# A hybrid convolution and delta-rule layer: the mixer's intermediates move to PSUM banks, the decay series to VectorE, and the planner learns of a shared SBUF way

## The chip, the cores and the metric

The kernel runs on one core of a Trainium2 chip, in one launch. The metric is device time in microseconds (us), the median of several runs; one more execution was profiled. The engines are TensorE (PE), VectorE (DVE), ScalarE (ACT), GpSimd (POOL) and SyncE (SP, which issues most transfers).

## The reference

One layer over 2048 tokens of width 1024, in fp32: a modulated RMS norm, a mixer, a residual, a second norm, a gated feed-forward part, a final norm. The change touches the mixer:

```python
h = adaln(x, g_norm_mix[layer], shift_m, scale_m)
p = h @ w_in[layer]
gate_b, gate_c, h_conv, q, k, v, z, a, bt = jnp.split(p, split_at, axis=-1)
ya = gate_b * causal_depthwise_conv(gate_c * h_conv, conv_w_mix[layer])      # 3 taps
...                                                  # ya: RMS norm by groups of 64
qkv = jax.nn.silu(causal_depthwise_conv(jnp.concatenate([q, k, v], axis=-1), conv_w_qkv[layer]))  # 4 taps
...                                                  # q, k normalised; 4 heads of 128
beta = jax.nn.sigmoid(bt)
g_dec = -jnp.exp(a_log[layer]) * jax.nn.softplus(a + dt_bias[layer])
o = chunked_gated_delta_rule(q, k, v, g_dec, beta)
o = rms_norm(o, g_dn_out[layer]) * jax.nn.silu(z)
y = jnp.concatenate([ya, o], axis=-1) @ w_out[layer]
x = x + gate_m[:, None, :] * y
```

The delta rule keeps a 128x128 state for each head and steps over chunks: `v_new = u - w @ state`, `o = q @ state + attn @ v_new`, `state = state * exp(g_last) + k.T @ v_new`, where u and w come from the inverse of a unit lower triangular matrix for each chunk.

## The kernel before

A matrix product in fp32 is made of three fast ones (fp32r): high part by high, high by low, low by high. `split_w` makes `whi` (ACT cast) and `wlo` (DVE difference) of each weight strip; `scale_split` makes `hTh` and `hTl` of the normed, transposed rows. So a projection of a strip is 24 matmuls of 128x512 (`proj`, `dmm`), and these fill PE.

The mixer runs in four blocks of 512 tokens. A block projects four strips each of k, q, v and z, then 12 strips for the convolution half, and ends in the out-projection: two halves of 512 columns, each over four pairs of strips in the order `KPS`, where `ya` are the convolution's rows and `ybs` (tiles `ym`) the delta rule's. The first result of each four chunks of `ybs` is needed in the second pair of the first half. During it the next block's rows are transposed (`transpose_split`, pool `kq`).

Beside the projections, generators ("chains") issue all else. `head_chain` turns 16 columns of a and b (`ab2`), computes the decay g by a softplus series on [128 x 16] tiles, issues three small matmuls on g (L880 to L882), then one pair of matmuls on products `rg` for each head (L896), then `kT`'s. It goes on to a block inverse by recursion on DVE and transfers through DRAM. `level_chain` completes the inverse, `chunk_chain` steps over the chunks (`R`, `W`, `state`, `o`), `out_chain` norms o and turns it back (L1135). `mix_chain` norms the convolution half, `second_norm` reads the block before back, norms and turns it (L565), `mod_gen` and `to_row` (L485) make the modulation vectors, whose weight sums run on DVE (L444).

PSUM has eight banks in two pools of four, `pd` for projections and `pm` for the rest. `cv`, `lv` and `ch` are pools of SBUF tiles which chains take and give back.

What stands where is decided while the program is built. `Clock` estimates when each instruction ends: `fit` places it in a gap of its engine, `note` has the costs. After each third matmul `tick` resumes every chain whose next inputs `due` estimates as ready, plus 0.3 us. From the q strips of block 0 on, until the mixer's last out-projection, `order` and `pin` fix every engine's queue by the estimated start. Engines run their queues in order; transfers wait in SP's queue.

Of the kernel before, what the change touches and what calls it, by code (L numbers as in the profile page):

```python
# [53 lines left out]
class Clock:  # L54
# [15 lines left out]
    def fit(self, name, ready, cost):  # L70

        gaps = self.gaps[name]
        while len(gaps) > 1 and gaps[0][1] < self.pe - 60:
            gaps.pop(0)
        n = next(n for n, (a, b) in enumerate(gaps) if max(a, ready) + cost <= b)
        a, b = gaps[n]
        s = max(a, ready)
        gaps[n:n + 1] = [g for g in ([a, s], [s + cost, b]) if g[1] - g[0] > 0.02]
# [47 lines left out]
    def note(self, i):  # L126
# [9 lines left out]
        if op == "DMACopy":  # L136
            cost = min(a.free_size() * a.partition_size() for a in outs + ins) * 4 / 240e3
            begin = self.fit(eng, start, 0.45) - 0.45
            end = self.fit("DMA", begin + 1.2, cost) + 0.8
# [13 lines left out]
        else:  # L153
            if "Activation" in eng:
# [46 lines left out]
def layer_kernel(ctx, tc, x, c, w_ada, b_ada, w_ada_final, b_ada_final, g_norm_mix, g_norm_ffn, g_norm_final,  # L201
# [335 lines left out]
    def scale_split(ps, k, gcol, scol, hh, hl):  # L537
        ht = sp.tile([P, BLK], F32, name="ht", bufs=2)
        nc.scalar.activation(ht, ps, AF.Identity, scale=gcol[:, k:k + 1], bias=scol[:, k:k + 1])
        nc.vector.tensor_copy(hh[:, k, :], ht)  # L540
        nc.vector.tensor_sub(hl[:, k, :], ht, hh[:, k, :].bitcast(F32))  # L541
# [13 lines left out]
    def second_norm(b):  # L555
        for i in range(CH):
# [4 lines left out]
            for q in range(2):  # L561
                yield xt,
# [100 lines left out]
    with ExitStack() as actx:  # L663
        ap_ = Split(rctx, actx, {"hTh", "hTl", "kq", "kd", "vt", "zs", "E", "X", "lv", "ch", "Dg", "state"},
                    {"halo0", "halo1", "uhalo0", "uhalo1", "strict_r", "gones_r", "junkd", "nk", "nq", "sk",
# [117 lines left out]
        for b in range(NB):  # L783
# [18 lines left out]
            junkd = ap_.tile([P, BLK], mybir.dt.bfloat16, name="junkd")  # L802
# [28 lines left out]
            def head_chain(ps, b=b):  # L831
# [26 lines left out]
                nc.gpsimd.tensor_mul(zz, sg, sg)
                pl = t16("sp_p")
                nc.gpsimd.tensor_scalar(pl, zz, 1.0 / 17, 1.0 / 15, op0=ALU.mult, op1=ALU.add)  # L860
                for n in (13, 11, 9, 7, 5, 3, 1):
                    nc.gpsimd.tensor_mul(pl, pl, zz)
                    nc.gpsimd.tensor_scalar_add(pl, pl, 1.0 / n)
                nc.gpsimd.tensor_mul(pl, pl, sg)
                nc.scalar.activation(sy, sy, AF.Relu)
# [3 lines left out]
                nc.gpsimd.tensor_mul(g, pl, brd(nexpa))
# [16 lines left out]
                for h in range(NH):  # L886
# [6 lines left out]
                    yield tuple(rgs)  # L893
# [174 lines left out]
            def chunk_chain():  # L1068
# [5 lines left out]
                for j in range(CH):  # L1074
# [8 lines left out]
                    else:  # L1083
# [8 lines left out]
                        nc.vector.tensor_mul(R, h4(pks), bc(e_g, P))  # L1092
                        nc.vector.tensor_sub(R, vt[:, j], R)
# [25 lines left out]
            def out_chain(j, o):  # L1119
# [3 lines left out]
                for h in range(NH):  # L1123
                    nc.scalar.activation(junkd[:, hsl[h]], o[:, h, :], AF.Square, accum_out=so[:, h:h + 1])
# [7 lines left out]
                yield from take("ch", 1)  # L1132
# [3 lines left out]
                oT = ch_tile([P, NH, P])  # L1136
                nc.vector.scalar_tensor_tensor(oT, h4(pot), col["g_dn"], zs[:, :, j * P:(j + 1) * P],
# [17 lines left out]
            for key, c0, dstT in (("k", 2048, kT), ("q", 1536, qT), ("v", 2560, None)):  # L1155
                clock.pinned = clock.pinned or key == "q"
                for h in range(NH):
# [9 lines left out]
                    cb = ap_.tile([P, BLK + 3], F32, name="cb", bufs=2)  # L1167
                    nc.scalar.copy(cb[:, 3:], ps)
                    nc.vector.tensor_copy(cb[:, 0:3], halo[:, m, :])
# [3 lines left out]
                    tap = [col["cw_qkv"][:, t * 12 + m:t * 12 + m + 1] for t in range(4)]  # L1173
                    nc.vector.tensor_scalar_mul(cv, cb[:, 0:BLK], tap[0])
# [638 lines left out]
```

## Time and profile before

| | us |
|---|---|
| median of 3 runs | 2469.59 |
| lowest, highest | 2467.96, 2475.31 |
| profiled execution, time | 2471.74 |
| profiled execution, span | 2470.0 |
| PE busy | 2358.7 |
| DVE busy | 1809.0 |
| ACT busy | 1043.2 |
| POOL busy | 654.8 |

The span goes from the first to the last instruction; 1.7 us of the time lie around it. The mixer takes about the first 1140 us, the feed-forward part the rest. A row of waits names the waiting engine and line, who was waited for, the total, the times and the longest. A row of instructions has line, engine, operation, output and inputs with shape and count, then busy us and mean ns of one, then idle time before them. In a row of the timeline the start and the duration stand first, and in brackets the idle time before it.

### The profile page before, as it was taken

Reading aid. Unit: us, or ns where it says so; the run is one execution under the profiler, and the core shown is the slowest. Engines: PE = TensorE matmul, PEld = TensorE weight load, DVE = VectorE, ACT = ScalarE, POOL = GpSimd, SP = SyncE. Lnnn points to the kernel's source line nnn. Section 1 sums busy time; section 2 is a strip of 40 time slices with the busy share of each in tenths; the row PEclk is TensorE's granted clock in tenths of the full one; section 3 lists DMA queues with packets and bytes.
Section 4 is the critical chain, followed back from the end, with each engine's and each line's share of the span. In section 5 each row is a group of like instructions: output and inputs, shape, how many; then the busy total and the mean of one; then the engine's idle time right before and its main releaser. Section 6 shows DMA issues by size and latency. Waiting matters only on the chain. (4 is left out here: it accounts for less than half of the span.)

```text
span 2470.0 us, 30843 instructions
## 1 busy us (share of the span) xinstructions
PE 2358.7 (95%) x11243; PEld 1946.5 (79%) x11243; DVE 1809.0 (73%) x2609; ACT 1043.2 (42%) x1801; POOL 654.8 (27%) x719
## 2 busy tenths in 40 slices
PE   5899999999999999998999999999999999999997
PEld 4778877888778877886878888878888877887786
DVE  6898759875897749778565655976556558878887
ACT  3533556343643555346543333533333323322345
POOL 2532246032731255122000000000000036444448
PEclk9999999999999999999999999999999999999999
DMA  7442445624562444336673332854333365333433
GB/s 245 114 112 62 146 140 171 171 89 134 144 161 59 145 136 107 77 107 192 180 252 111 105 116 86 252 158 119 110 91 112 102 219 176 115 107 130 132 126 146
DMA packets 397535, 336.98 MB, mean 136 GB/s; under 512 B 39476, under 2 KB 338749, under 8 KB 397383
## 3 DMA queue, kind: packets, MB, share of 16 engines
q1 hardware_dynamic: 397126, 334.91, 44.5%
q8 instruction: 88, 1.44, 0.2%
q14 instruction: 65, 0.52, 0.1%
q10 hardware_dynamic: 256, 0.10, 0.0%
HBM read 261.55 MB, written 73.41 MB: 136 GB/s over the span
## 5 line engine op out<-in xcount | busy, mean ns | idle before, releaser
L378 ACT CAST whi<-wraw 128x1024 fp32r<-128x1024 f32 x278 | 291.8, 1050 | 383.9 <-PE pd L311 194.9
L380 DVE TENSOR_TENSOR wlo<-wraw,whi 128x1024 fp32r<-128x1024 f32 x275 | 344.5, 1253 | 100.1 <-ACT whi L378 93.6
L311 PE MATMUL pd<-hTh,whi 128*128 128x512 f32 x896 | 371.3, 415 | 1.1 <-DVE hTh L540 1.1
L311 PE MATMUL pd<-hTl,whi 128*128 128x512 f32 x896 | 356.5, 398 | 1.1 <-DVE hTl L541 1.1
L311 PE MATMUL pd<-hTh,wlo 128*128 128x512 f32 x896 | 356.6, 398 | 0.6 <-DVE wlo L380 0.5
L1487 POOL TENSOR_TENSOR wraw<-wraw 128x1024 f32<-128x1024 f32 x2 | 4.8, 2402 | 779.7 <-DMA wraw<-in_w_down_dram 779.7
L311 PEld LDWEIGHTS pd<-hTh,wlo 128*128 128x128 f32 x896 | 172.2, 192 | 39.1 <-DVE wlo L380 1.5
L311 PEld LDWEIGHTS pd<-hTh,whi 128*128 128x128 f32 x896 | 172.6, 193 | 35.3 <-DVE hTh L540 2.6
L311 PEld LDWEIGHTS pd<-hTl,whi 128*128 128x128 f32 x896 | 172.7, 193 | 33.9 <-DVE hTl L541 2.2
L1441 DVE TENSOR_TENSOR sg<-sg,pd 128x512 f32<-128x512 f32 x44 | 30.2, 686 | 171.6 <-PE pd L311 171.6
L1681 DVE TENSOR_TENSOR acc<-acc,pd 128x512 f32<-128x512 f32 x192 | 127.3, 679 | 31.6 <-PE pd L311 31.5
L1564 ACT CAST xh<-ra 128x640 fp32r<-128x640 f32 (+1 forms) x88 | 62.3, 719 | 187.4 <-PE pm L311 147.8
L1176 DVE SCALAR_TENSOR_TENSOR cv<-cb,pcb,cv 128x512 f32<-128x512 f32 x144 | 137.7, 956 | 3.7
L1573 POOL TENSOR_TENSOR xl<-ra,xh 128x640 fp32r<-128x640 f32 (+1 forms) x40 | 66.1, 1652 | 164.8 <-ACT xh L1564 164.8
L1281 POOL TENSOR_TENSOR cv<-cv 128x512 f32<-128x512 f32 x32 | 45.1, 1419 | 209.5 <-DVE cv L1280 119.6
L1681 DVE TENSOR_TENSOR acc<-acc,pm 128x512 f32<-128x512 f32 x120 | 81.6, 680 | 18.3 <-PE pm L311 17.6
L311 PE MATMUL pd<-whi,ym 128*128 128x512 f32 x256 | 87.2, 401 | 0.0
L1610 POOL TENSOR_TENSOR wraw<-wraw 128x512 f32<-128x512 f32 x40 | 70.0, 1772 | 40.5 <-DMA wraw<-in_w_down_dram 40.4
L311 PE MATMUL pd<-S2h,whi 128*128 128x512 f32 x176 | 69.3, 394 | 4.8 <-ACT whi L378 4.8
L311 PE MATMUL pd<-A22h,whi 128*128 128x512 f32 x176 | 69.6, 395 | 3.5 <-DVE sg L1441 3.5
L311 PE MATMUL pm<-S4h,whi 128*128 128x512 f32 x176 | 68.7, 390 | 1.8 <-ACT sg L1435 1.8
L311 PE MATMUL pd<-S3h,t3h 128*128 128x512 f32 x176 | 69.2, 393 | 0.4 <-ACT sg L1427 0.3
(457 smaller groups left out, 6347.7 us busy)
## 6 DMA issues: line engine op xcount, KB each, us to landing
wraw<-in_w_in_dram SPq DMA_DIRECT2D x112, 512.0 KB, 4.4
wraw<-in_w_gate_up_dram SPq DMA_DIRECT2D x88, 512.0 KB, 4.1
ra<-act SPq DMA_DIRECT2D x80, 448.0 KB, 4.3
act<-S SPq DMA_DIRECT2D x80, 256.0 KB, 2.4
act<-act SPq DMA_DIRECT2D x68, 256.0 KB, 2.2
wraw<-in_w_ada_dram SPq DMA_DIRECT2D x32, 512.0 KB, 3.8
wraw<-in_w_out_dram SPq DMA_DIRECT2D x32, 512.0 KB, 3.7
wraw<-in_w_down_dram SPq DMA_DIRECT2D x22, 512.0 KB, 3.6
```

Of the source, the lines that this page charges most:

```text
L311: mm(*args, **kw)
L378: nc.scalar.copy(hi, raw)
L380: (lo_engines.popleft() if lo_engines else nc.vector).tensor_sub(lo, raw, hi.bitcast(F32))
L1176: nc.vector.scalar_tensor_tensor(cv, cb[:, t:t + BLK], tap[t], cv, op0=ALU.mult, op1=ALU.add)
L1281: nc.gpsimd.tensor_add(xr, xr, yo)
L1441: nc.vector.tensor_add(s5[i], s5[i], a[i])
L1487: nc.gpsimd.tensor_mul(r, r, first_w["gate"])
L1564: nc.scalar.copy(hi, raw[:, c0:c1, :])
L1573: eng.tensor_sub(lo, raw, hi.bitcast(F32))
L1610: nc.gpsimd.tensor_mul(r[:, hs], r[:, hs], gate_f[:, hs])
L1681: nc.vector.tensor_add(accs[s, u][:, ns], accs[s, u][:, ns], ps)
```

## The change

Six things. (1) The convolutions read the projection in its PSUM bank; the values that reach over the block's edge are kept apart (`edge`, `uedge`), multiplied for the next block on POOL (`halo_terms`) and added to the first columns. (2) `scale_split` scales in place in PSUM, casts on ACT, and DVE takes the difference from PSUM. (3) The chunk correction `R` and the turned output `oT` are formed in their PSUM banks. (4) The softplus series runs on DVE. (5) In the out-projection x is loaded into `cb`, not `cv`, and the sum is formed in `yo`. (6) The planner counts a shared way ("port") for POOL and for DVE instructions with two SBUF inputs or a fast single one, and its slack before a chain goes on is 3.0 us in `second_norm`, 0.6 for `rg`, 2 more in `settled`.

```diff
+            needs, near = [eng], [a for a in ins if "PSUM" not in str(a.space) and a.free_size() > 1]
...
-                cost = 0.14 + n * 1.7e-3 + (0.42 if n < 200 else 0.6) * self.busy("EngineType.DVE", start)
+                cost = 0.16 + n * 1.7e-3
+                if near:
+                    needs.append("port")
...
+                if len(near) > 1 or near and len(wide) < 2 and op in ("TensorScalarPtr", "TensorCopy"):
+                    needs.append("port")
                 cost = a + n * b / 1e3
-            end = self.fit(eng, start, cost)
+            end = self.fit(needs, start, cost)
...
-        return max([clock.next_free("pm", banks + low), *(clock.ready(t) for t in w)]) + 0.3
+        late, w = (w[0], w[1:]) if isinstance(w[0], float) else (0.3, w)
+        return max([clock.next_free("pm", banks + low), *(clock.ready(t) for t in w)]) + late
...
-        while clock.pinned and due(tiles, 0) > clock.pe:
+        while clock.pinned and due(tiles, 0) + 2 > clock.pe:
...
     def scale_split(ps, k, gcol, scol, hh, hl):
-        ht = sp.tile([P, BLK], F32, name="ht", bufs=2)
-        nc.scalar.activation(ht, ps, AF.Identity, scale=gcol[:, k:k + 1], bias=scol[:, k:k + 1])
-        nc.vector.tensor_copy(hh[:, k, :], ht)
-        nc.vector.tensor_sub(hl[:, k, :], ht, hh[:, k, :].bitcast(F32))
+        nc.scalar.activation(ps, ps, AF.Identity, scale=gcol[:, k:k + 1], bias=scol[:, k:k + 1])
+        nc.scalar.copy(hh[:, k, :], ps)
+        nc.vector.tensor_sub(hl[:, k, :], ps, hh[:, k, :].bitcast(F32))
...
-                yield xt,
+                yield 3.0, xt
...
-                nc.gpsimd.tensor_scalar(pl, zz, 1.0 / 17, 1.0 / 15, op0=ALU.mult, op1=ALU.add)
-                for n in (13, 11, 9, 7, 5, 3, 1):
-                    nc.gpsimd.tensor_mul(pl, pl, zz)
-                    nc.gpsimd.tensor_scalar_add(pl, pl, 1.0 / n)
+                nc.vector.tensor_scalar_mul(pl, zz, 1.0 / 17)
+                for n in (15, 13, 11, 9, 7, 5, 3):
+                    nc.vector.scalar_tensor_tensor(pl, pl, 1.0 / n, zz, op0=ALU.add, op1=ALU.mult)
...
-                    yield tuple(rgs)
+                    yield 0.6, *rgs
...
-                        nc.vector.tensor_mul(R, h4(pks), bc(e_g, P))
-                        nc.vector.tensor_sub(R, vt[:, j], R)
+                        nc.vector.tensor_mul(h4(pks), h4(pks), bc(e_g, P))
+                        nc.vector.tensor_sub(R, vt[:, j], h4(pks))
...
-                oT = ch_tile([P, NH, P])
-                nc.vector.scalar_tensor_tensor(oT, h4(pot), col["g_dn"], zs[:, :, j * P:(j + 1) * P],
+                oT = h4(pot)
+                nc.vector.scalar_tensor_tensor(oT, oT, col["g_dn"], zs[:, :, j * P:(j + 1) * P],
...
+            def conv(cv, u, taps, back):
+                n = len(taps) - 1
+                nc.vector.tensor_scalar_mul(cv, u, taps[n])
+                for t in range(n - 1, -1, -1):
+                    nc.vector.scalar_tensor_tensor(cv[:, n - t:], u[:, :BLK - n + t], taps[t], cv[:, n - t:],
+                                                   op0=ALU.mult, op1=ALU.add)
+                nc.vector.tensor_add(cv[:, :n], cv[:, :n], back)
...
-                    nc.scalar.copy(cb[:, 3:], ps)
-                    nc.vector.tensor_copy(cb[:, 0:3], halo[:, m, :])
-                    nc.vector.tensor_copy(nhalo[:, m, :], ps[:, BLK - 3:])
...
-                    nc.vector.tensor_scalar_mul(cv, cb[:, 0:BLK], tap[0])
-                    for t in (1, 2, 3):
-                        nc.vector.scalar_tensor_tensor(cv, cb[:, t:t + BLK], tap[t], cv, op0=ALU.mult, op1=ALU.add)
+                    conv(cv, ps, [col["cw_qkv"][:, t * 12 + m:t * 12 + m + 1] for t in range(4)], halo[:, m, :])
+                    nc.scalar.copy(edge[:, m, :], ps[:, BLK - 3:])
...
-                    xr = cv_tile([P, 512])
+                    xr = ap_.tile([P, BLK], F32, name="cb", bufs=2)
                     nc.sync.dma_start(xr, x[row * P:(row + 1) * P, ns])
                     yo = cv_tile([P, 512])
                     nc.vector.tensor_mul(yo, pso[t], gate_m[:, ns])
-                    nc.gpsimd.tensor_add(xr, xr, yo)
-                    nc.sync.dma_start(x1d[row][:, ns], xr)
+                    nc.gpsimd.tensor_add(yo, yo, xr)
+                    nc.sync.dma_start(x1d[row][:, ns], yo)
```

**The order, decay in block 0, PE.** The matmuls on g are L880 to L882, L889 to L891 after the change; L896, now L905, are the first head's matmuls on `rg`. L311, now L321, are projections. Before:

```order
L311 MATMUL pd<-hTl,whi 128x512
L311 MATMUL pd<-hTh,wlo 128x512
L880 MATMUL pm<-g,ck 128x16
L881 MATMUL pm<-g,ones_r 128x16
L882 MATMUL pm<-g,ck 128x16
L311 MATMUL pd<-hTh,whi 128x512
```

After:

```order
L321 MATMUL pd<-hTh,wlo 128x512
L889 MATMUL pm<-g,ck 128x16
L890 MATMUL pm<-g,ones_r 128x16
L891 MATMUL pm<-g,ck 128x16
L905 MATMUL pm<-lv,strict_r 128x512 x2
L321 MATMUL pd<-hTh,whi 128x512
```

Between the transposes of `ab2` and g PE has 33 projections, before 45, and the first head's `rg` matmuls follow at once, where 12 projections stood between. In blocks 1 to 3 there are 39 projections up to g, before 78, and in all of them 9 more up to the first `rg` matmuls, before 12.

**Decay in block 0, DVE.** `sp_s`, `sp_z`, `sp_p` are the series' tiles, `cv` a convolution, `wlo` a weight's low part, `wraw<-wraw,cs` a weight sum. Before, where only the reciprocal L855 belongs to the series:

```order
L380 TENSOR_TENSOR wlo<-wraw,whi 128x1024
L855 RECIPROCAL sp_s<-sp_s 128x16
L1170 COPY halo_511<-pd 128x3
L1174 TENSOR_SCALAR cv<-cb,pcb 128x512
L1169 COPY cb<-halo_152 128x3
L1176 SCALAR_TENSOR_TENSOR cv<-cb,pcb,cv 128x512
```

After:

```order
L868 TENSOR_TENSOR sp_s<-sp_s,sp_e 128x16
L390 TENSOR_TENSOR wlo<-wraw,whi 128x1024
L870 TENSOR_TENSOR sp_z<-sp_s 128x16
L1160 SCALAR_TENSOR_TENSOR cv<-pd,pcb,cv 128x510
L872 TENSOR_SCALAR sp_p<-sp_z 128x16
L1158 TENSOR_SCALAR cv<-pd,pcb 128x512
L874 SCALAR_TENSOR_TENSOR sp_p<-sp_p,sp_z 128x16
L1160 SCALAR_TENSOR_TENSOR cv<-pd,pcb,cv 128x509
```

In block 0 another instruction of DVE stands between each two steps of the series. In blocks 1 to 3 the series' 17 steps stand in one piece, behind the four last gated rows (L1298) of the block before, a split, a weight sum and the copy of a and b.

**The end of block 0, PE.** L1135, now L1143, turns the last chunk's o; L1116 and L1118 are the matmuls for the state and for o; `ym` marks out-projection. Before:

```order
L311 MATMUL pd<-hTl,whi 128x512
L311 MATMUL pd<-hTh,wlo 128x512
L1135 MATMUL pm<-ck,ch 128x128 x4
L311 MATMUL pd<-hTh,whi 128x512
L311 MATMUL pd<-hTl,whi 128x512
```

After:

```order
L1116 MATMUL pm<-ch,kd 128x128 x4
L1118 MATMUL pm<-ch,E 128x128 x4
L321 MATMUL pd<-whi,ym 128x512
L321 MATMUL pd<-wlo,ym 128x512
L321 MATMUL pd<-whi,ym 128x512 x2
L321 MATMUL pd<-wlo,ym 128x512
L321 MATMUL pd<-whi,ym 128x512 x2
L321 MATMUL pd<-wlo,ym 128x512
L321 MATMUL pd<-whi,ym 128x512
L1143 MATMUL pm<-ck,ch 128x128 x4
L321 MATMUL pd<-whi,ym 128x512
```

Before, the last transposes stood 27 projections ahead of the out-projection. Now they stand in it, 9 matmuls behind the product that they wait for, and the last six matmuls of that pair of strips, which read their result, follow. The completion of the inverse by `level_chain` begins 90 projections later in this block, in the others at about the same place or up to 21 matmuls earlier.

More of the change, by code (lines that the diff above doesn't have):

```diff
@@ L68, in __init__, with fit @@
         self.func, self.fast, self.pinned, self.kept = None, None, False, set()
[L70 to L78, printed above, removed]
+    def fit(self, names, ready, cost):
+        s, old = ready, None
+        while s != old:
+            old = s
+            for name in names:
+                gaps = self.gaps[name]
+                while len(gaps) > 1 and gaps[0][1] < self.pe - 60:
+                    gaps.pop(0)
+                s = next(max(a, s) for a, b in gaps if max(a, s) + cost <= b)
+        for name in names:
+            gaps = self.gaps[name]
+            n = next(n for n, (a, b) in enumerate(gaps) if a <= s and s + cost <= b)
+            a, b = gaps[n]
+            gaps[n:n + 1] = [g for g in ([a, s], [s + cost, b]) if g[1] - g[0] > 0.02]
         return s + cost
-    def busy(self, name, t):
-        return not any(a <= t < b for a, b in self.gaps[name])
     @staticmethod
@@ L137, in note @@
             cost = min(a.free_size() * a.partition_size() for a in outs + ins) * 4 / 240e3
-            begin = self.fit(eng, start, 0.45) - 0.45
-            end = self.fit("DMA", begin + 1.2, cost) + 0.8
+            begin = self.fit([eng], start, 0.45) - 0.45
+            end = self.fit(["DMA"], begin + 1.2, cost) + 0.8
             self.order(eng, begin, i)
@@ L794, in layer_kernel @@
             nuh = ap_.tile([P, 4, 2], F32, name=f"uhalo{(b + 1) % 2}")
+            edge = ap_.tile([P, 12, 3], F32, name="edge")
+            uedge = ap_.tile([P, 4, 2], F32, name="uedge")
             kT = ap_.tile([P, NH, BLK], F32, name="kq", bufs=2)
@@ L801, in layer_kernel @@
             zs = ap_.tile([P, NH, BLK], F32, name="zs")
-            junkd = ap_.tile([P, BLK], mybir.dt.bfloat16, name="junkd")
+            junkd = ap_.tile([P, P], mybir.dt.bfloat16, name="junkd")
             nk, nq, sk, bk, rq = (ap_.tile([P, NH, CH], F32, name=n) for n in ("nk", "nq", "sk", "bk", "rq"))
@@ L823, in sumsq @@
                     js = slice(j * P, (j + 1) * P)
-                    nc.scalar.activation(junkd[:, js], ps[:, js], AF.Square, accum_out=acc[:, h, j:j + 1])
+                    nc.scalar.activation(junkd, ps[:, js], AF.Square, accum_out=acc[:, h, j:j + 1])
             def wait(key, n):
@@ L1131, in out_chain @@
                 yield o,
-                yield from take("ch", 1)
                 pot = misc_ps()
@@ L1142, in out_chain, with halo_terms @@
                 nc.vector.tensor_sub(ybl, oT, ybh.bitcast(F32))
-                give("ch", 2)
+                give("ch", 1)
                 clock.kept.discard(o.name)
                 ybs.append((ybh, ybl))
+            def conv(cv, u, taps, back):
[5 more added lines that the diff above has]
+                nc.vector.tensor_add(cv[:, :n], cv[:, :n], back)
+            def halo_terms(sums, raw, taps):
+                k, n = raw.shape[1:]
+                taps = taps.rearrange("p (t m) -> p t m", m=k)
+                part = ap_.tile([P, k, n], F32, name="et")
+                for i in range(n):
+                    tap = taps[:, i, :].unsqueeze(2).to_broadcast([P, k, n - i])
+                    nc.gpsimd.tensor_mul(part[:, :, i:] if i else sums, raw[:, :, i:], tap)
+                    if i:
+                        nc.gpsimd.tensor_add(sums[:, :, :n - i], sums[:, :, :n - i], part[:, :, i:])
             if b:
@@ L1183, in layer_kernel @@
             spawn(chunk_chain(), 1)
+            halo_terms(nhalo, edge, col["cw_qkv"])
             for h in range(NH):
```

45 lines of the change are left out of this document (19 added, 26 removed).

## The prediction

> **What bounds the kernel now.** First the page's busy table, then the list of waits of TensorE (PE) and the rows of its timeline behind the longest.
>
> ```profile
> span 2470.0 us, 30843 instructions
> PE 2358.7 (95%) x11243; PEld 1946.5 (79%) x11243; DVE 1809.0 (73%) x2609; ACT 1043.2 (42%) x1801; POOL 654.8 (27%) x719
> ```
>
> PE works 2358.7 of 2470.0 us. The change removes no matmul, so it can win only in the 111 us in which PE waits, and in matmuls that run slowly after a wait. Who is waited for (total, times, longest):
>
> ```profile
> PE pm L880 <- POOL g L869: 20.1, 4, 8.6
> PE pm L565 <- ACT wraw L560: 5.2, 2, 3.6
> PE pm L818 <- DVE E L1036: 3.4, 2, 2.9
> PE pd L311 <- DVE cv L1280: 3.2, 2, 2.2
> PE pm L896 <- POOL lv L891: 2.9, 2, 1.5
> PE pm L818 <- DVE cb L1169: 2.5, 2, 2.3
> PE pm L485 <- DVE wraw L480: 2.3, 1, 2.3
> ```
>
> One wait stands out: once in each of the four blocks PE waits for the decay g, the end of GpSimd's (POOL) series. The timeline shows these waits in brackets; the rows by stretches of 10 us show what follows them, in the column with the granted clock, third from the end.
>
> ```profile
> 81.45 0.61 PE L880 MATMUL pm<-g,ck 128*128 128x16 f32 x2 [8.56 <-POOL g L869]
> 354.25 0.61 PE L880 MATMUL pm<-g,ck 128*128 128x16 f32 x2 [3.79 <-POOL g L869]
> 631.92 0.61 PE L880 MATMUL pm<-g,ck 128*128 128x16 f32 x2 [3.63 <-POOL g L869]
> 908.47 0.61 PE L880 MATMUL pm<-g,ck 128*128 128x16 f32 x2 [4.09 <-POOL g L869]
> 962.65 1.11 PE L565 MATMUL pm<-ck,wraw 128*128 128x128 f32 x4 [3.65 <-ACT wraw L560]
> ...
> 350.00:360.00 10.00, 6.21 (x20) 4.82 (x19) 1.93 (x5) 4.22 (x7) 8.84 (x20) 0.70 0.20 69
> 630.00:640.00 10.00, 8.07 (x27) 6.72 (x28) 2.81 (x4) 6.53 (x9) 9.21 (x16) 0.66 0.01 3
> 900.00:910.00 10.00, 5.91 (x27) 4.83 (x26) 7.63 (x13) 3.82 (x7) 8.74 (x17) 0.85 0.36 96
> 910.00:920.00 10.00, 10.00 (x41) 8.15 (x42) 4.35 (x6) 7.57 (x11) 7.14 (x7) 0.81 0.41 123
> 960.00:970.00 10.00, 7.34 (x29) 6.30 (x30) 9.82 (x15) 5.07 (x7) 9.09 (x8) 0.66 0.34 95
> ```
>
> After a wait of 3.6 us or more the clock falls. What it costs is (1 - clock) x 10 us: 3.0 after the wait at 354, 3.4 at 632, 1.5 + 1.9 at 908, 3.4 at 963. A wait of 4 us thus costs over 7.
>
> **The decay series in blocks 1 to 3: 21 us won.** The series is slow on POOL and short on VectorE (DVE), and its place on PE moves too.
>
> ```profile
> L863 POOL TENSOR_SCALAR sp_p<-sp_p 128x16 f32<-128x16 f32 x28 | 16.4, 586 | 2.5
> ...
> 165.13 0.21 DVE L946 TENSOR_TENSOR lv<-yal 128x30 f32<-128x30 f32 x1
> 165.37 0.21 DVE L948 TENSOR_TENSOR yal<-yal,lv 128x30 f32<-128x30 f32 x1
> ...
> 331.15 0.42 PE L838 MATMUL pm<-ck,cv 16*128 16x16 f32 x4
> 332.07 0.40 PE L311 MATMUL pd<-hTh,wlo 128*128 128x512 f32 x1
> 338.23 0.39 PE L311 MATMUL pd<-hTh,wlo 128*128 128x512 f32 x1
> ...
> 333.48 0.21 ACT L865 ACTIVATE sp_y<-sp_y 128x16 f32<-128x16 f32 x1
> ```
>
> The loop's seven additions alone (L863) take 16.4 / 4 = 4.1 us a block, and as many products stand between them. On DVE a small step that depends on the one before starts 0.24 us after it (165.13 to 165.37), and 13 stand between the exponential and g: 3.1 us. ScalarE's (ACT) part ends 2.2 us after the small transposes (333.48 + 0.21 against 331.15 + 0.42); in the new order its exponentials follow each other. So g is there about 2.2 + 0.2 + 3.1 = 5.5 us after the transposes. PE comes to g 39 projections later (78 before); they cost 0.228 us each (332.07 to 338.23 is 27 steps), so 8.9 us. The wait goes, with 3.4 us to spare: 3.79 + 3.63 + 4.09 = 11.5 us, and 3.0 + 3.4 + 3.4 = 9.8 us of clock. In front of the series on DVE stand four evictions of the block before; if they are late, the 3.4 us shrink.
>
> **The same in block 0: 4 us lost** (-3 to +7). There DVE's series alternates with convolutions and weight splits, and PE has 33 projections (7.5 us) up to g instead of 45. Between the first step and g stand 7 convolution steps, 4 splits, a weight sum, 2 scalings and 2 edge adds:
>
> ```profile
> L380 DVE TENSOR_TENSOR wlo<-wraw,whi 128x1024 fp32r<-128x1024 f32 x142 | 181.9, 1281 | 55.0 <-ACT whi L378 50.9 <-DMA cv<-in_x_dram 2.8 <-PE pm L1206 1.2
> L1176 DVE SCALAR_TENSOR_TENSOR cv<-cb,pcb,cv 128x512 f32<-128x512 f32 x144 | 137.7, 956 | 3.7
> L1137 DVE SCALAR_TENSOR_TENSOR ch<-pm,pcb,zs 128x512 f32<-128x512 f32 x16 | 11.9, 744 | 4.9 <-PE pm L1135 4.9
> L444 DVE SCALAR_TENSOR_TENSOR wraw<-wraw,cs 128x1024 f32<-128x1024 f32 x28 | 39.4, 1407 | 0.7 <-DMA wraw<-in_w_ada_dram 0.7
> L1174 DVE TENSOR_SCALAR cv<-cb,pcb 128x512 f32<-128x512 f32 x48 | 27.9, 582 | 1.6 <-POOL cv L1281 1.6
> ...
> L1681 DVE TENSOR_TENSOR acc<-acc,pd 128x512 f32<-128x512 f32 x192 | 127.3, 679 | 31.6 <-PE pd L311 31.5
> L378 ACT CAST whi<-wraw 128x1024 fp32r<-128x1024 f32 x278 | 291.8, 1050 | 383.9 <-PE pd L311 194.9
> ```
>
> An instruction starts some 0.08 us before the one ahead has ended, so 7 x 0.67 + 4 x 1.2 + 1.33 + 2 x 0.6 + 2 x 0.1 = 12.2 us, and 15 small steps in the gaps, at half of 0.24, 1.8. ACT's part ends 2.2 us and one cast (L378, 1.05) after the transposes. So g falls at 17.3 us, a wait of 9.8 where 8.56 stands. The first decay matmuls now follow at once, and POOL's two products for them need over 1 us each: 2.4 more. Together 12.2, some 4 worse.
>
> **The convolutions: 7.5 us won on PE.** Per q, k or v strip go one ACT copy, two edge copies on DVE and the SBUF source; come an edge copy on ACT and an edge add on DVE, and for all strips of a block eight small POOL products and sums, which a POOL at 27% hides. No row shows the convolution's step from PSUM. The nearest is L1137, PSUM in, 0.744 us; the upper bound is L1176's 0.956. I take 0.744: 144 x 0.21 = 30 us of DVE work. What makes L1176 dear is POOL beside it: L1681, PSUM in, stays at 0.679 over 192 in a stage where POOL works. The other edits (the first scaling rises from 0.58 to some 0.68, edges and hT casts leave, the series comes, 17 x 0.24 us a block) about balance. DVE's lateness is three waits, 3.4 + 2.5 + 3.2 = 9.1; I credit 7.5.
>
> [...]
>
> **Row scaling: 3.5 us won at the start** (0 to 6). The cast moves to ACT, and DVE's difference reads PSUM. In the opening DVE's operations are drawn out beside POOL's weight splits:
>
> ```profile
> 29.74 0.78 ACT L539 ACTIVATE ht<-pm,Sm,Gm 128x512 f32<-128x512 f32 x1 [2.49 <-DVE Sm L731]
> ...
> 34.49 2.73 DVE L541 TENSOR_TENSOR hTl<-ht,hTh 128x512 fp32r<-128x512 f32 x1
> 42.16 1.28 DVE L541 TENSOR_TENSOR hTl<-ht,hTh 128x512 fp32r<-128x512 f32 x2
> ...
> L1141 ACT CAST ym<-ch 128x512 fp32r<-128x512 f32 x16 | 9.9, 616 | 19.6 <-DVE ch L1137 19.6
> ```
>
> From 29.74 ACT needs five scalings at 0.70, three strip casts at 0.97 and five casts at 0.54, 9.1 us; with DVE's last difference the row is done at 39.5, against 42.16 + 1.28 = 43.4 now. Of these 4 us I credit 3.5. In later blocks ACT needs 1.24 us per row tile, about what PE gives it (a tile's transposes and three matmuls); the out-projection hides it, and without that cover it costs under 1 us a block.
>
> **The planner: 14 us won.** The slack of 3.0 us covers L565 (5.2 and 3.4 of clock), 0.6 us and the earlier g cover L896 (2.9), 2 us more cover L485 (2.3): 13.8.
>
> **The end of block 0: 10 us lost** (4 to 14). The inverse starts 90 projections later there, so the last chunk's output runs into the out-projection: its transposes stand 9 matmuls (2.0 us) behind the output that they turn.
>
> ```profile
> L1124 ACT ACTIVATE junkd<-ch 128x128 bf16<-128x128 f32 x64 | 19.0, 298 | 47.1 <-DVE ch L1116 38.7 <-DVE ch L1113 8.4
> L506 POOL TENSOR_TENSOR so<-so,mhalf 128x4 f32<-128x4 f32 x16 | 19.4, 1214 | 1.3
> L1129 POOL TENSOR_TENSOR ch<-ch,so 128x512 f32<-128x512 f32 x16 | 20.7, 1292 | 1.3
> ```
>
> The way is two sums at 0.68, four squares (1.2 and their reads), POOL's 1.2 + 1.3 and four short ones: over 6 us, so PE waits 4. Then DVE's 0.74, ACT's 0.62 and DVE's 0.68 with their signals pass before the next out-projection matmul, 2.6 more. The next block's row transposes and projections are queued behind them on PE, so nothing hides this: 7 us, and 3 of clock as after the waits above. On SP's queue the transfer that ends the inverse now stands just ahead of the output weights, three strip loads later than before; PE's chain ends there all the same.
>
> **The rest.** Chunk corrections and outputs in PSUM keep their operations and only hold banks longer; the new output adds wait for x in `cb`, two buffers, as the two pairs of `cv` did. I count 4 us for waits that the new order makes and no row shows (0 to 15; three blocks today have some 2 us each of waits under 1 us).
>
> Sum: -21.3 + 4 - 7.5 - 3.5 - 13.8 + 10 + 4 = -28.1. The profiled execution took 2471.7 us, 2.1 above the median of the runs, 2469.6: 2443.6 against it, 2441.5 on the median's scale. I say 2441.
>
> **Rivals.** *Residues (2453):* g is late by 2 us in blocks 1 to 3 after all, with 2 of clock each, 12 in all. For it: DVE's four evictions in front; against it the 3.4 us. 0.16. *Little left over (2420):* block 0's end costs nothing (-10), its g is no later than now (-4), the lateness goes whole (-1.6) and the new order makes no waits (-4). For it: today's three later block ends have no long wait; against it: the 9 matmuls. 0.15. *DVE becomes the bound (2465):* a strip needs 0.68 + 3 x 0.744 + 0.2 = 3.1 us of convolution, 1.28 of split and 1.41 of weight sum, 5.8, or 6.4 at 0.956, against PE's 24 x 0.228 = 5.5; at 0.45 over the 36 strips with a weight sum that is 16 us, and the 7.5 go unwon. For it: that sum; against it: the 1.28 and 1.41 are means in which POOL's disturbance lies. [...] 0.10. *Slower:* the series queues behind evictions and convolutions on DVE in every block as in block 0. Each us past the slack of 3.4 costs PE 1 us in each of three blocks and brings the clock down again, so from about 12 us late the gain is gone; at 17 late it is 2485. For it: one queue, in order; against it: in blocks 1 to 3 the series stands in one piece. 0.07. *The new order's waits equal the old ones (2470):* 0.05.
>
> My forecast keeps 0.47, with 2430 to 2450 as its own range. 0.3% is 7.4 us, about what a measurement can tell. Faster: 0.47 + 0.16 + 0.15 and part of the DVE case, 0.83; same 0.09; slower 0.08. The range 2417 to 2465 leaves out the slower cases and the far side of the good one.
>
> **What would show it.** The waits for g gone at three blocks and left, about 10 us, in block 0; L565's, L896's and L485's gone; DVE's convolution step near 0.74; a new wait of some 4 us at the transposes of the last chunk of block 0 and one behind it. Wrong would be the forecast if TensorE's busy time grew, if g were late in blocks 1 to 3, or if PE waited for banks that a convolution holds.

## The result, and the profile after

The changed kernel takes 2440.2 us (median of 4 runs, 2438.67 to 2442.49), the kernel before 2470.6 beside it: ratio 0.9876, 95% interval 0.9858 to 0.9893. The forecast was 2441. The page's span and busy times:

```profile
span 2439.4 us, 30808 instructions
PE 2344.2 (96%) x11243; PEld 1935.6 (79%) x11243; DVE 1769.4 (73%) x2577; ACT 1044.8 (43%) x1841; POOL 592.6 (24%) x655
```

PE is busy 14.5 us less and idle 16.1 us less. DVE lost 40 us of work, POOL 62. The list of PE's waits (total, times, longest), where the rows named in the forecast stand, and the timeline's rows of the long ones:

```profile
PE pd L321 <- DVE cv L1298: 10.5, 2, 8.1
...
PE pm L1143 <- POOL ch L1138: 6.6, 4, 5.7
PE pm L889 <- DVE g L878: 6.5, 1, 6.5
...
PE pd L321 <- ACT ym L1149: 1.5, 1, 1.5
PE pm L905 <- POOL lv L900: 1.3, 2, 1.0
...
PE pm L574 <- ACT y L569: 0.7, 1, 0.7
```

```profile
76.74 0.61 PE L889 MATMUL pm<-g,ck 128*128 128x16 f32 x2 [6.49 <-DVE g L878]
279.31 1.11 PE L1143 MATMUL pm<-ck,ch 128*128 128x128 f32 x4 [5.72 <-POOL ch L1138]
281.90 0.80 PE L321 MATMUL pd<-whi,ym 128*128 128x512 f32 x1 [1.47 <-ACT ym L1149]
1091.24 0.50 PE L321 MATMUL pd<-whi,yah 128*128 128x512 f32 x1 [2.38 <-DVE cv L1298]
1101.65 0.79 PE L321 MATMUL pd<-whi,yah 128*128 128x512 f32 x1 [8.14 <-DVE cv L1298]
```

The wait for g, 20.1 us in four blocks before, is left in block 0 alone. The waits of `second_norm`'s transposes (L565, now L574; the expectations below call them two-row products) and of `to_row`'s column sums (L485) are gone or small. New are the last chunk's transposes of block 0 (279), as forecast, and a wait of 8.1 us where the mixer hands over to the feed-forward part (1101), which the forecast did not have. The rows below are the stretches around these two, with the granted clock third from the end. By stretches of 1 us it reads 0.50 from 277 to 286 and from 1093 to 1105; with the parts at their ends the trace has 10.2 us at half clock at the wait at 279, and 13.7 at those at 1091 and 1101:

```profile
280.00:290.00 10.00, 8.53 (x37) 6.67 (x36) 4.03 (x5) 5.84 (x9) 0.16 (x1) 0.67 0.00 0
1090.00:1100.00 10.00, 2.27 (x6) 1.32 (x6) 1.19 (x2) 1.05 (x2) 2.96 (x2) 0.60 0.69 209
1100.00:1110.00 10.00, 8.35 (x28) 6.73 (x29) 9.64 (x11) 6.85 (x11) 3.50 (x2) 0.71 0.71 234
```

Where the time went is read by places in PE's queue: both kernels issue 11243 matmuls, so the time from the start of one numbered matmul to that of another is taken in both (a number can be another matmul where an order differs, so the places are rough at their ends). The column "before" is that time in us; the columns behind it are each run's change from it. The runs e2 to e11 are told below.

| matmuls, place | before | after | e2 series | e5 convolutions | e8 slacks | e4 no shared way | e11 old planner |
|---|---|---|---|---|---|---|---|
| 0 to 260: start, decay of block 0 | 92.9 | -0.1 | +0.6 | -4.4 | -0.9 | -1.6 | -1.7 |
| to 600: block 0, projections | 74.3 | -8.6 | -1.6 | -9.2 | 0.0 | -8.4 | -7.6 |
| to 1500: block 0's end | 163.7 | +10.6 | 0.0 | +0.4 | -0.1 | -0.5 | -0.9 |
| to 3000: block 1 | 291.9 | -13.5 | -1.7 | -8.2 | +3.7 | -11.4 | -9.6 |
| to 4300: block 2 | 253.2 | -12.3 | +5.8 | -8.3 | +4.9 | -4.3 | -8.6 |
| to 5500: block 3 | 231.6 | -13.4 | -2.9 | -4.2 | +1.4 | -9.8 | -9.9 |
| to 5750: handover | 68.6 | +10.9 | +1.0 | +1.7 | +2.1 | +2.3 | +3.9 |
| sum of these | 1176.2 | -26.4 | +1.2 | -32.2 | +11.1 | -33.7 | -34.4 |
| to the last: feed-forward | 1275.0 | -4.3 | -8.2 | -6.3 | -4.8 | +3.4 | -2.0 |

The feed-forward part differs by up to 8 us between profiles even where an edit leaves its code and planner alone (e2, e5), so the sum above it is the one to read. Two profiles of the changed kernel agree better: e12 has -25.8 and -3.8 where the table has -26.4 and -4.3. What moves the feed-forward part was not found.

### The profile page after: what moved, and what is told of

Its sections match the earlier page's. It is cut to its first block, busy times and chain, and to the rows that moved or that the text cites. A ratio compares the mean times of both kernels' runs of the same rounds, so it can differ in the third digit from the quotient of the medians.

```text
span 2439.4 us, 30808 instructions
## 1 busy us (share of the span) xinstructions
PE 2344.2 (96%) x11243; PEld 1935.6 (79%) x11243; DVE 1769.4 (73%) x2577; ACT 1044.8 (43%) x1841; POOL 592.6 (24%) x655
## 5 line engine op out<-in xcount | busy, mean ns | idle before, releaser
L390 DVE TENSOR_TENSOR wlo<-wraw,whi 128x1024 fp32r<-128x1024 f32 x275 | 339.6, 1236 | 109.3 <-ACT whi L388 101.7
L321 PE MATMUL pd<-hTh,whi 128*128 128x512 f32 x896 | 365.2, 408 | 3.5 <-ACT hTh L549 2.6
L321 PE MATMUL pd<-hTl,whi 128*128 128x512 f32 x896 | 351.6, 392 | 2.7 <-DVE hTl L550 2.7
L321 PE MATMUL pd<-hTh,wlo 128*128 128x512 f32 x896 | 351.7, 392 | 0.0
L321 PEld LDWEIGHTS pd<-hTh,whi 128*128 128x128 f32 x896 | 169.7, 190 | 36.4 <-ACT hTh L549 2.7
L321 PEld LDWEIGHTS pd<-hTh,wlo 128*128 128x128 f32 x896 | 169.2, 189 | 36.5
L321 PEld LDWEIGHTS pd<-hTl,whi 128*128 128x128 f32 x896 | 170.0, 190 | 34.2 <-DVE hTl L550 3.1
L1160 DVE SCALAR_TENSOR_TENSOR cv<-pd,pcb,cv 128x511 f32<-128x511 f32 (+2 forms) x176 | 131.5, 747 | 4.9
L1299 POOL TENSOR_TENSOR cv<-cv,cb 128x512 f32<-128x512 f32 x32 | 52.2, 1644 | 164.7 <-DVE cv L1298 140.3
L321 PE MATMUL pd<-whi,ym 128*128 128x512 f32 x256 | 87.9, 404 | 1.5 <-ACT ym L1149 1.5
L321 PE MATMUL pd<-S2h,whi 128*128 128x512 f32 x176 | 69.5, 395 | 3.1 <-ACT whi L388 3.1
L321 PE MATMUL pd<-S3h,t3h 128*128 128x512 f32 x176 | 69.0, 392 | 2.9 <-ACT sg L1445 2.9
L321 PE MATMUL pd<-S2h,wlo 128*128 128x512 f32 x176 | 69.6, 396 | 2.2 <-DVE wlo L390 2.2
L321 PE MATMUL pd<-A22h,whi 128*128 128x512 f32 x176 | 69.6, 395 | 2.3 <-DVE sg L1459 2.2
```

Of the source, the lines that this page charges most:

```text
L321: mm(*args, **kw)
L390: (lo_engines.popleft() if lo_engines else nc.vector).tensor_sub(lo, raw, hi.bitcast(F32))
L1160: nc.vector.scalar_tensor_tensor(cv[:, n - t:], u[:, :BLK - n + t], taps[t], cv[:, n - t:], op0=ALU.mult, op1=ALU.add)
L1299: nc.gpsimd.tensor_add(yo, yo, xr)
```

## The experiments

Each time has its own runs of the kernel before beside it (2466.6 for e1 to e4, 2468.3 for e5 to e8, 2468.0 for e9 to e12); ratios are to that. The planner builds the queues anew for each kernel, so an edit can also change the order.

### Which part carries the gain: e2, e5, e6

**e2, the series alone on DVE:**

```diff
-                nc.gpsimd.tensor_mul(pl, pl, zz); nc.gpsimd.tensor_scalar_add(pl, pl, 1.0 / n)
+                nc.vector.scalar_tensor_tensor(pl, pl, 1.0 / n, zz, op0=ALU.add, op1=ALU.mult)
```

> The kernel before with the decay series alone on VectorE; planner, convolutions, scaling and outputs as before. TensorE comes to g 60 projections after the transposes in blocks 1 to 3 (13.7 us; g needs about 5.5). Theory: the three waits and their half clock go, 21.7 us, and block 0 changes by under 5: 2446 to 2452 us. Rival (without the lighter VectorE of the changed kernel the series stands behind convolutions and evictions there and g stays late): 2460 to 2470 us, with the waits for g still in the list.

Measured: 2466.9 us, ratio 1.0 (0.9991 to 1.0009). Its waits of PE:

```profile
PE pm L565 <- ACT wraw L560: 7.2, 4, 3.9
PE pm L818 <- DVE E L1034: 6.7, 2, 4.8
...
PE pm L878 <- DVE g L867: 4.3, 1, 4.3
PE pd L311 <- DVE wlo L380: 4.0, 4, 2.0
PE pm L1033 <- DVE vt L1063: 3.8, 1, 3.8
PE pm L818 <- DVE vt L1063: 3.4, 1, 3.4
```

The three waits for g went, as the forecast said, and nothing was won: DVE is late elsewhere instead (`E`, `vt`, the weights' low parts, and at `second_norm`'s transposes L565).

**e5, the convolutions alone from PSUM**, with their edges and halo terms as in the change; the copy of each strip on ACT goes with it:

```diff
-                    nc.scalar.copy(cb[:, 3:], ps)
...
-                        nc.vector.scalar_tensor_tensor(cv, cb[:, t:t + BLK], tap[t], cv, op0=ALU.mult, op1=ALU.add)
+                    conv(cv, ps, [col["cw_qkv"][:, t * 12 + m:t * 12 + m + 1] for t in range(4)], halo[:, m, :])
```

> The kernel before with the convolutions alone reading PSUM (edges on ScalarE, halo terms on GpSimd); decay series on GpSimd, planner, scaling and outputs as before. TensorE comes to g 78 projections after the small transposes, as before. New theory (the convolutions' operations on SBUF slowed both VectorE and GpSimd: with them in PSUM the series on GpSimd took 7.2 us instead of 12.3 to 12.9): g is there 5 us earlier than before, where it was 3.6 to 4.1 us late, so the three waits and their half clock go (21.7 us) with the series still on GpSimd, and VectorE's lateness shrinks by 5 to 9: 2436 to 2440 us against 2466.6 before. Rival (the sum of the forecast: convolutions are worth 7.5, the waits for g need the series on VectorE): 2459 us.

Measured: 2435.2 us (2432.9 to 2437.72), ratio 0.9865 (0.9847 to 0.9883): as much as the whole change gained, with the series still on POOL. Its waits of PE, then one row of the groups on POOL (the series' additions):

```profile
PE pm L882 <- POOL g L871: 6.4, 4, 2.4
...
PE pm L565 <- ACT wraw L560: 0.6, 2, 0.4
```

```profile
L865 POOL TENSOR_SCALAR sp_p<-sp_p 128x16 f32<-128x16 f32 x28 | 10.0, 356 | 2.4
```

The additions take 356 ns instead of 586, and in blocks 1 to 3 the series runs 9.2 to 9.3 us instead of 12.3 to 12.9. PE comes to g where it came before and waits 2.4 us at most. The waits for column sums and for the first `rg` products, and nearly all of those for `E` and at `second_norm`'s transposes, went too, with no slack added. The edit has three effects at once: POOL's steps get shorter, DVE has 28 us less work (1781.3 for 1809.0) and ACT 17 less (1026.1 for 1043.2). No run parts these. That POOL's shorter steps shorten PE's waits is seen at g; how much of the 33 us they carry in all stays open.

**e6, convolutions and series together**, the two edits above.

> The kernel before with the convolutions reading PSUM and the decay series on VectorE; planner, scaling and outputs as before. New theory: the series' engine adds little once the convolutions are in PSUM, within 4 us of the run with the convolutions alone, so 2434 to 2442 us. Rival (additive terms of the forecast): 7.5 + 21.3 - 4 less than before: 2442 us, with the convolutions alone at 2459.

Measured: 2440.4 us, ratio 0.9884 (0.9868 to 0.99). Once the convolutions are in PSUM, moving the series brings nothing. By the ledger it loses in block 0: the first 260 matmuls take 0.2 us less than before, and in e5 4.4 less.

### The other way round: e1, e7

**e1, the changed kernel with the series back on POOL** (the reverse of e2's diff).

> The changed kernel with the decay series alone put back on GpSimd. TensorE now comes to g 57 projections after the small transposes in blocks 1 to 3 (39 in the changed kernel, 78 before). Theory (the series' engine is what took the three waits away): before, g came 3.6 to 4.1 us late at 78 projections; 21 projections x 0.228 us earlier it is 8.4 to 8.9 us late, three times, with about 4 to 5 us of half clock each: 36 to 41 us, so 2476 to 2481 us. Rival (the new order alone did it, and the engine of a 16-wide series does not matter): 2440 us, within 4.

Measured: 2445.8 us, ratio 0.9913 (0.99 to 0.9927). My theory of that time was off by over 30 us: the waits for g in blocks 1 to 3 did not come back. The series' additions on POOL, and its waits of PE:

```profile
L874 POOL TENSOR_SCALAR sp_p<-sp_p 128x16 f32<-128x16 f32 x28 | 8.0, 286 | 2.4
```

```profile
PE pm L1145 <- POOL ch L1140: 11.3, 3, 5.7
...
PE pm L891 <- POOL g L880: 5.2, 1, 5.2
```

POOL's series takes 7.2 us in these blocks (3.2 on DVE), and PE comes 57 projections after the transposes, when it is done. What e1 loses against the changed kernel is a second late end: the planner now sets block 1's last transposes beside the out-projection as well (5.1 and 1.5 us, with a 3.3 us wait ahead of them; block 1 costs +2.8 instead of -13.5). It wins some of that back at the handover (+2.4 instead of +10.9) and in the first 260 matmuls (-4.7 instead of -0.1).

**e7, the changed kernel with the convolutions back on the copy in SBUF** (the reverse of e5's diff).

> The changed kernel with the convolutions alone put back on a copy in SBUF (ScalarE's copy, VectorE's edge copies). Series on VectorE, planner, scaling, outputs as changed. The order then has the inverse late in blocks 0 and 1 (last chunk's transposes beside the out-projection in both). New theory (the convolutions in PSUM are what pays): VectorE is late again as in the kernel before with the series moved, some 20 to 25 us, and the end of block 1 costs 11 more: 2470 to 2478 us. Rival (additive terms): 7.5 and 11 for the end of block 1: 2458 us.

Measured: 2489.8 us, ratio 1.0078 (1.0061 to 1.0095), above both expectations. Its waits of PE:

```profile
PE pd L321 <- ACT ym L1147: 22.7, 10, 3.1
...
PE pm L1141 <- POOL ch L1136: 10.2, 3, 5.9
```

The waits for g stay away here too (series on DVE); the loss sits at the block ends, where the planner, which counts the SBUF convolutions on the shared way, puts the inverse late in blocks 0 and 1. The run thus mixes two causes, and I take from it only that the convolutions' place is worth some 50 us to the changed kernel, its order included.

### The planner: e8, e4, e11

**e8, the three slacks alone on the kernel before:**

```diff
+        late, w = (w[0], w[1:]) if isinstance(w[0], float) else (0.3, w)
...
+        while clock.pinned and due(tiles, 0) + 2 > clock.pe:
```

> The kernel before with the three slacks alone (3.0 us for the two-row products, 0.6 for the decay differences, 2 us for column sums). The forecast gave them 13.8 us in the changed kernel. If that holds alone: 2453 us against 2466.6. Rival (what the slack takes from one wait appears at the next, VectorE and GpSimd being late anyway): 2462 to 2468 us, with the waits of the two-row products gone from the list and others grown.

Measured: 2482.6 us, ratio 1.0056 (1.0041 to 1.0071): slower. Its waits of PE:

```profile
PE pm L881 <- POOL g L870: 19.1, 4, 8.0
...
PE pm L819 <- ACT cv L1178: 7.3, 2, 4.8
...
PE pm L819 <- DVE E L1037: 4.8, 2, 4.1
...
PE pm L486 <- ACT ht L568: 3.3, 1, 3.3
```

`second_norm`'s transposes no longer wait; PE waits for `cv`, `E` and at the column sums (L486 here) instead, and the wait for g stands. The slack only chose who waits.

**e4, the changed kernel without the shared way in the estimate:**

```diff
-                if near:
-                    needs.append("port")
+                cost = 0.14 + n * 1.7e-3 + (0.42 if n < 200 else 0.6) * self.busy("EngineType.DVE", start)
```

> The changed kernel with the planner's old costs: no shared SBUF way, the old fixed surcharge for GpSimd; the three slacks and all operations stay as changed. The order then has block 0's inverse at projection 483 (579 in the changed kernel, 489 before) and the last chunk's transposes at 666 (714). Theory: the waits of 5.7 and 1.5 us at the end of block 0 and their half clock (10.2 us) go: 10 to 11 us won, 2429 to 2431 us, if the places of the other blocks cost no more than now. Rival (the shared way in the estimate is what keeps the rest of the order right): new waits of 1 us and more in blocks 1 to 3, 2440 us or above.

Measured: 2438.7 us, ratio 0.989 (0.9877 to 0.9904). The theory held at its place: block 0's end costs -0.5 instead of +10.6, and the handover +2.3 instead of +10.9. But those 20 us did not arrive: blocks 1 to 3 give back 13.7 (waits for `kT` of 2.2 and 2.5 us, one of 3.3 for `lv`), and the feed-forward part reads 7.7 longer. So the shared way in the estimate wins nothing: in the mixer the changed kernel is 7.3 us better without it (-33.7 for -26.4), and in the whole time nothing is seen of it.

**e11, all the change's operations with the planner as before** (the reverse of e4's and e8's edits), and **e12, the changed kernel once more beside it.**

> All operations of the changed kernel (convolutions and row scaling in PSUM, series on VectorE, chunk corrections and outputs in PSUM) with the planner as before: no slacks, no shared SBUF way in the estimate. Theory (the planner's edits bring nothing together): within 4 us of the changed kernel or faster, 2432 to 2441 us. Rival (the forecast's 13.8 us for the slacks are real once VectorE is light): 2449 to 2454 us, with waits of PE for the two-row products (L565's) and the column sums in its list.

> The changed kernel once more, as reference for the two runs beside it: 2438 to 2441 us. If the convolutions alone carry the change, the run with convolutions and row scaling alone is at or below it; by the forecast's terms it would be some 20 us above it.

Measured: e11 2434.9 us (2430.97 to 2436.64), ratio 0.9857 (0.984 to 0.9875); e12 2442.3 us (2440.88 to 2444.33), ratio 0.989 (0.9871 to 0.9909). The runs do not overlap: the planner's edits cost some 7 us in time, and 8 or 9 in the mixer by the ledger. One wait of e11 is what the slack was for:

```profile
PE pm L564 <- ACT wraw L559: 8.6, 3, 3.2
```

The slack does take it away (0.7 in the changed kernel), and it brings nothing: e4 has the slacks and e11 has not, and their sums in the mixer are -33.7 and -34.4. What the changed kernel loses at block 0's end and at the handover is missing in e4 too, so it goes with the shared way and not with the slacks. e11 beats the changed kernel beside it. The runs of e5 lie below the changed kernel's as well, but with a reference of their own, and the intervals of the ratios overlap.

### The handover: e3

```diff
-                    nc.gpsimd.tensor_add(yo, yo, xr)
+                    nc.vector.tensor_add(yo, yo, xr)
```

The reason for the wait at 1101 is a chain over four queues. In the changed kernel's timeline, one row each of POOL, of SP's queue, of ACT and of DVE:

```profile
1082.31 9.41 POOL L1299 TENSOR_TENSOR cv<-cv,cb 128x512 f32<-128x512 f32 x1 [19.98 <-DVE cv L1298]
```

```profile
1091.74 0.34 SPq L1300 DMA_DIRECT2D x<-cv  x1
...
1093.15 1.00 SPq L593 DMA_DIRECT2D A22h<-xT  x2
```

```profile
1098.95 0.81 ACT L594 ACTIVATE A22h<-A22h,Sf,Gf 128x512 f32<-128x512 f32 x1 [9.52 <-DMA A22h<-xT]
```

```profile
1100.31 0.69 DVE L590 TENSOR_TENSOR S4l<-A22l,S4h 128x512 fp32r<-128x512 f32 x1 [9.11 <-ACT S4h L589]
1100.91 0.68 DVE L1298 TENSOR_TENSOR cv<-pd,gate_m 128x512 f32<-128x512 f32 x1
```

POOL's sum takes 9.41 us where 1.29 is usual, beside 14 DVE operations without a gap. The last of these, L1298, reads a bank; the 13 ahead of it read two tiles in SBUF, and the sum ends 1.13 us after the last of them. The store of its result holds SP's queue; the loads of `xT` behind it are issued 1.4 us after the sum ends; ACT waits for them with the cast `S4h` behind; DVE waits for that cast with the output product L1298 behind; and PE waits for the bank that L1298 empties.

> The changed kernel with the sum of output and x (L1299) on VectorE instead of GpSimd. Theory: where the mixer hands over to the FFN, one such sum on GpSimd took 9.41 us (1.29 elsewhere) beside an unbroken run of VectorE operations; the store behind it held SP's queue, the loads of xT came late, and TensorE waited 2.4 and 8.1 us and ran at half clock for 13.7 us. With the sum on VectorE the store goes out at once: those waits go but for 2 to 3 us, about 10 us won, 2 us given back for 32 sums of 0.69 us on VectorE: 2430 to 2433 us. Rival (the xT loads or VectorE's own queue are late at that place for another reason): the wait stays, 2440 to 2444 us.

Measured: 2433.8 us (2428.71 to 2434.47), ratio 0.9862 (0.9847 to 0.9877). The wait of 8.1 us is gone, one of 4.4 is left, and the handover costs +2.6 instead of +10.9; in the ledger the rest of the mixer stays within 1.1 us at each place. In time the interval overlaps the changed kernel's. Another order does as much: in e4 and e11 the sum stays on POOL, in e4 it takes 2.9 us at most, and the handover costs +2.3 and +3.9.

```profile
L1290 POOL TENSOR_TENSOR cv<-cv,cb x32: 1262/1296/2875, 287.3 to 1121.0; 128x512 f32<-128x512 f32 x32
```

This row is of e4 (shortest, median and longest in ns).

### Row scaling, and VectorE beside GpSimd: e10, e9

**e10, e5 with the row scaling in PSUM as well** (the diff of `scale_split`).

> The kernel before with two edits: convolutions reading PSUM (as in e5) and the row scaling kept in PSUM with its cast on ScalarE. TensorE's order is that of e5. The forecast gave the row scaling 3.5 us at the start: 2431 to 2432 us if that holds. Rival (the start is no sooner done, since what is not drawn out on VectorE queues on ScalarE, and later blocks pay for ScalarE's casts): 2435 to 2438 us.

Measured: 2442.9 us (2440.81 to 2443.57), ratio 0.989 (0.9875 to 0.9906). Against e5 the start is 1.7 us shorter, block 0's end 2.8 longer, the feed-forward part, which the edit does not touch, 5.0 longer. So the row scaling wins at the start half of what was forecast and nothing in all; whether it costs 2 us or 8 stays open. The run equals e12 (2442.3), the changed kernel, as the expectation there has it if the convolutions carry the change; by the forecast's terms it would lie some 20 us above.

The parts (3) and (5) of the change ran only together with all the rest (e11), so what they are worth is not shown.

**e9, VectorE's forms beside GpSimd's.** The kernel holds these operations alone and ran once. GpSimd's work all ended within the first 56 us, so it lay beside stretches of 8, 4 and 7 operations, and the runs of 30 were alone.

> Nothing of the layer is computed: 30 back-to-back operations of VectorE on 128x512 in three forms (sum of two SBUF tiles, the convolution's step from SBUF, the convolution's step from PSUM), each beside 4 independent sums of 128x512 on GpSimd and beside a chain of 16 steps of 128x16 on GpSimd, and each alone. Theory (an engine's claim on SBUF's shared way shuts the other out): beside an unbroken run of VectorE's sums a GpSimd sum ends only when the run ends (up to 18 us, 1.3 alone); beside the step from PSUM both run as alone (GpSimd 1.3 us and 0.22 us a tiny step, VectorE 0.74 us). The step from SBUF: VectorE 0.96 and a tiny step 0.4 to 0.6 when both run. Rival (the two only share a rate): a GpSimd sum takes at most twice as long, 2.6 us, beside any of them, and PSUM makes no difference.

Measured, from the timeline; `dv<-a` is the sum of two SBUF tiles, `dv<-a,dv` the convolution's step from SBUF, `dv<-ps,a,dv` the step from PSUM, `pg` GpSimd's sums, `tiny` its small steps:

```profile
6.87 9.16 DVE L241 TENSOR_TENSOR dv<-a 128x512 f32<-128x512 f32 x8
7.54 5.06 POOL L253 TENSOR_TENSOR pg<-a 128x512 f32<-128x512 f32 x3
18.94 4.74 DVE L245 SCALAR_TENSOR_TENSOR dv<-a,dv 128x512 f32<-128x512 f32 x4
20.77 0.69 POOL L257 TENSOR_SCALAR tiny<-tiny 128x16 f32<-128x16 f32 x1
32.45 4.69 DVE L249 SCALAR_TENSOR_TENSOR dv<-ps,a,dv 128x512 f32<-128x512 f32 x7
32.52 1.27 POOL L253 TENSOR_TENSOR pg<-a 128x512 f32<-128x512 f32 x1
33.75 0.26 POOL L257 TENSOR_SCALAR tiny<-tiny 128x16 f32<-128x16 f32 x1
55.93 15.13 DVE L241 TENSOR_TENSOR dv<-a 128x512 f32<-128x512 f32 x25
90.28 19.29 DVE L245 SCALAR_TENSOR_TENSOR dv<-a,dv 128x512 f32<-128x512 f32 x29
130.44 19.18 DVE L249 SCALAR_TENSOR_TENSOR dv<-ps,a,dv 128x512 f32<-128x512 f32 x29
```

Alone, DVE's sum takes 15.13 / 25 = 0.61 us; beside GpSimd 9.16 / 8 = 1.15, and GpSimd's 5.06 / 3 = 1.69 for 1.27. The step from SBUF takes 4.74 / 4 = 1.19 beside GpSimd and GpSimd's small step 0.69; the step from PSUM 4.69 / 7 = 0.67 and the small step 0.26, in a stretch where GpSimd never paused. Alone the two steps take 19.29 / 29 = 0.67 and 19.18 / 29 = 0.66. In these stretches, beside GpSimd's sums and small steps, both engines were slowed together where DVE read two tiles in SBUF, and neither where it read one of them in PSUM. That a sum on GpSimd would wait for the end of the whole run was not seen here; the longest took 1.78 us. This is what the runs show of the planner's shared way.

## Why the prediction was right, and where it was not

The total and the sign hold, and the changed kernel's trace shows the waits where the steps put them, but for the handover. What carries the gain is another part than the one credited with it: the sum treated as separate terms what the runs showed to be, for the most part, one cause. That it came out within 1 us of the time is luck: 21.3 us for the series and 13.8 for the slacks, which alone won nothing, stood in for convolutions that alone won 33.

- **Convolutions, 7.5 us.** One row of the page's groups, the convolution's step after the change:

```profile
L1160 DVE SCALAR_TENSOR_TENSOR cv<-pd,pcb,cv 128x511 f32<-128x511 f32 (+2 forms) x176 | 131.5, 747 | 4.9
```

The step was sized right (0.747 us; 0.744 forecast) and its worth wrongly: 33 us in e5. The part of the prediction that went wrong is "DVE's lateness is three waits", of which it credited 7.5 us: having said that POOL beside it makes L1176 dear, it asked only what POOL costs DVE and not what DVE's reads from SBUF cost POOL. PE's waits for g, 20.1 us on POOL's series, were left out of this term, and in e5 they fall to 6.4. The quoted rows had a sign of it, L863 with 586 ns for a step on [128 x 16]; e9 shows such a step at 0.25 to 0.26 us where DVE reads only one tile from SBUF.
- **Decay series in blocks 1 to 3, 21.3 us.** What the changed kernel does there was forecast to 0.1 us. In DVE's timeline of block 1 the first and the last operation of the series, and PE's first matmul on g:

```profile
329.75 0.11 DVE L866 TENSOR_SCALAR sp_s<-sp_e 128x16 f32<-128x16 f32 x1
...
332.77 0.18 DVE L878 TENSOR_TENSOR g<-sp_p,nexpa 128x16 f32<-128x16 f32 x1
```

```profile
336.32 0.29 PE L889 MATMUL pm<-g,ck 128*128 128x16 f32 x2
```

The series takes 3.2 us (3.1 forecast) and is 3.4 us ahead of PE (3.4 forecast). But the term is not the series' own: alone it brings nothing (e2), and without it most of those waits go as well (e5, e1).

- **The series in block 0, 4 us lost.** A wait of 6.5 us and 1.3 for the products, where 9.8 and 2.4 were forecast and 8.56 stood before; with the half clock behind it the place is about even, since the first 260 matmuls take 0.1 us less than before. Beside kernels that differ in the series alone the loss is there: 4.6 us against e1, and 4.2 in e6 against e5. The convolutions, 4.4 us faster there in e5, hide it.
- **Row scaling, 3.5 us.** 1.7 at the start, and not kept (e10).
- **Planner slacks, 13.8 us.** The waits did go, and the time did not: alone the slacks cost 14 us (e8), and in the changed kernel they bring nothing (e4 beside e11). What failed is crediting a wait with its length: moving an order makes someone else wait, and most of these waits go with the convolutions anyway.
- **The end of block 0, 10 us lost.** 5.7 and 1.5 us of wait and half of 10.2 us at half clock make 12.3; the ledger has 10.6 at this place. e4 shows its cause, the shared way in the estimate.
- **New waits, 4 us.** Those at the handover alone, of 2.4 and 8.1 us, cost 10.9. Most of it came from an operation that the forecast left at its price, the sum on POOL: with the sum on DVE 2.6 are left (e3).

So the table has -21.7 for the waits for g in blocks 1 to 3 (11.5 idle and half of 20.5 us at half clock, 6.8 at each wait; by stretches of 1 us the clock reads 0.50 from 354 to 360, 631 to 637 and 907 to 913), -26 for all else that shrank before the handover, and +21.5 at two places; the forecast had -21.3, -24.8 and +18. That the convolutions alone take away most of the first two, it did not see. Of the rivals, "DVE becomes the bound" comes closest to what e2 shows, where the convolutions stay in SBUF.

The forecast took the convolution's step to be no dearer from its bank than from a copy in SBUF, and the runs agree: 0.747 us against 0.956 a step and 33 us in all (e5), and in e9 the step takes 0.66 to 0.67 us from either place while GpSimd is still. Beside the step from SBUF the same small step of GpSimd takes 0.69 us in e9, beside the step from PSUM 0.26.

## What to carry to other kernels

Where two engines are both late, price each edit by what it does to the other engine too: an operand moved from SBUF to PSUM here sped up work on GpSimd that the edit never touched (356 ns for 586 a step of the series in e5). Do not add up waits as terms: run each part alone and all but each part, since two parts can remove the same wait and a slack in the order can only choose who waits. A long operation in the trace that is short elsewhere (9.41 for 1.29 us) is worth following through the queues behind it, because a store that waits for it held the loads behind it in the same queue here (those of `xT` went out 1.4 us after the sum's end).

## What the runs showed of the hardware

- Beside POOL's sums, with small steps between them, DVE and POOL slowed one another in two of the three forms run in e9, those where DVE read two SBUF tiles: 1.15 to 1.19 us for 0.61 to 0.67 on DVE, 1.69 for 1.27 and 0.69 for 0.26 on POOL; beside the step from PSUM both kept their times (0.67 us on DVE, 1.27 and 0.26 on POOL).
- One sum on POOL took 9.41 us through 14 back-to-back operations of DVE that kept their own times (0.69 us at 512 columns). It ended 1.13 us after the last of 13 operations with two SBUF tiles, which is near its whole time alone (1.26 to 1.29); how far it ran before that, no run shows. In e12, the same kernel, the chain behind it came again: the store at 1092.53 and the loads of `xT` at 1093.94 (1091.74 and 1093.15 in the profile above), and waits of PE of 2.7 and 7.3 us. In e9 both engines went on side by side instead, each slower (1.69 for 1.27 us and 1.15 for 0.61). What decides between the two was not found.
